# Four column orders for the moving operand of the down-projection products

## The chip, the cores and the metric

The kernel runs on one core of one Trainium2 chip. The metric is the device time of one execution in microseconds, from launch to end, median of the runs; lower is better. Beside the runs there is one profiled execution, whose span (first to last instruction) is given with its views.

## What is computed

One layer of a hybrid encoder over 256 tokens of 2048 channels, in float32. Only its last step matters for this change, the MLP with a hidden width of 8192 and a squared ReLU:

```python
x = x + merged @ w_out[i]
h2 = rms_norm(x, norm2_g[i])
x = x + jnp.square(jax.nn.relu(h2 @ w_mlp_up[i])) @ w_mlp_down[i]
```

Everything ahead of it (state-space branch, attention branch, convolution branch, gates, their merge) is the same in both kernels.

## The kernel before

All weights stream through the core once. SyncE fetches them in units of 256 rows by 512 columns (tile `raw`, 512 kB, two rows of 512 float32 on each of 128 partitions, five buffers). ScalarE copies each unit to a tile `hi` in the type fp32r (line 1208), VectorE subtracts to get the remainder `lo` (line 255); both have four buffers. Activations have been split in the same way. A product of a unit is then three passes on TensorE: activations' high part times `hi`, activations' low part times `hi`, activations' high part times `lo`.

Eight units make a block, which accumulates in one PSUM tile `main` [128, 2, 512], two banks, one per token tile of 128 tokens. There are two such tiles, so block *b* needs block *b*-2 to have been read. Blocks come in two modes. In mode "W" the weights are the stationary operand and the activations move in matmuls of 256 columns (lines 1251, 1253, 1255). In mode "X" the activations are stationary (128 by 128, a new load for each matmul) and a row of the weight tile moves, 512 contiguous float32 per partition (lines 1260, 1261, 1263): twelve matmuls per unit, two rows times two token tiles times three passes.

The MLP comes last in the stream. It is cut into four rounds of 2048 hidden channels. A round is four up-projection blocks (mode "W"; `job_up` applies the ReLU and the square and makes the tiles `ah` and `al`) and four down-projection blocks (mode "X", `down_block`, `ah` and `al` stationary). `mlp_order` puts them in the order U0 U1 D0 U2 D1 U3 D2 D3, so the groups D0 to D3 of down blocks stand apart, but for the last two. A down block ends with two additions on VectorE, one per token tile, which read the bank and add it to the residual `x` (`oacc[i]`): line 1070 for the first three rounds, line 1074 for the last, where each addition is followed by the store of 128 by 512 outputs.

The program is written out in one fixed order. A scheduler class hands out the work beside the stream by estimated engine times; its estimates, and so the order, know nothing of the order in which a matmul reads its columns. TensorE executes its matmuls in program order and takes a weight load ahead of them.

Of the kernel before, what the change touches and what calls it, by code (L numbers as in the profile page):

```python
# [21 lines left out]
T = 256  # L22
D = 2048
# [17 lines left out]

# Slabs of 4 kB per partition and PSUM banks for the work beside the weight stream.
SLOTS = 33
BANKS = 4
# Pacing of that work, in ns of engine time: the largest credit in units of the gain per weight unit, the shares
# of DVE and ACT that the weights' splitting leaves, the credit and the slabs that late work keeps free, the slack
# of the estimated clocks, and the distance between two engines.
CAP = 1.2
# [7 lines left out]
WPRIO = 1  # L56
# Weight units that are split ahead of their products.
LEAD = 3
# [20 lines left out]
class Sched:  # L79
    """Issues work beside the weight stream in portions that the engines have time for."""  # L80

# [30 lines left out]
    def _try(self, j, force):  # L112
        """Advances the job by one request; False when it has to stay."""
        if j.req is None:
# [56 lines left out]
    def require(self, cond, what):  # L171
        """Runs jobs, the most urgent first, until the condition holds."""
        level = 0
        while not cond():
            moved = False
            for j in [x for x in self.jobs if x.prio <= level]:
                while not cond() and not j.done and self._try(j, True):
                    moved = True
                if cond():
                    break  # L180
            if moved:
                level = 0
            else:
                level += 1
                if level > 9:
                    raise RuntimeError("stuck: " + what + " " + str([(j.name, j.req) for j in self.jobs])
                                       + " mem %d banks %d" % (self.mem, self.banks))
# [3 lines left out]
def kernel(ctx: ExitStack, tc: tile.TileContext, xT, xn, par, cm, cd, cq, w1, wq, ws, out):  # L191
# [27 lines left out]

    # ------------------------------------------------------------ constants  # L220
    cpar = cp.tile([P, NPAR], F32, name="cpar")
# [23 lines left out]

    # ------------------------------------------------------------ small helpers
    def natural(ap):
        """tokens in order, seen in the order of the attention: the even ones before the odd ones."""
        return ap.rearrange("p (j r) -> p r j", r=2)
# [7 lines left out]
    def add4(acc, src, first):  # L257
        """adds the four chunks of a slab to acc."""
        for k in range(4):
            if first and k == 0:  # L260
                continue
            yield "g", 700
            G.tensor_tensor(acc, src[:, 0, :] if first and k == 1 else acc, src[:, k, :], op=ALU.add)  # L263

    def rstd_steps(dst, ms, n):
        """dst = ms ** -0.5, one Newton step after the tables."""
        s = small([n], f"rs{n}", bufs=2 if n < 64 else 1)
# [17 lines left out]
    def spread(r):  # L285
        """[token, tile] to a row of all tokens on every partition, in a bank."""
        yield "m", 1
# [12 lines left out]

    # ------------------------------------------------------------ startup: x * g, rms
    def prep(kc):
        """hi and lo parts of x*g for a chunk of channels."""
        src = xt[kc // 4][:, kc % 4, :]
# [34 lines left out]
    def job_h():  # L339
        """h = x*g*rstd and its parts, for the blocks after the first."""  # L340
        yield "j", lambda: "rbc1" in st
# [21 lines left out]

    # ------------------------------------------------------------ dt
    def job_dt(main):
# [78 lines left out]

    # ------------------------------------------------------------ q, k, v of one slot (3 heads)
    qkv = {}

    def job_qk(main, off, key, gain, scaled=False):
        """three heads of q or k: per-head RMS, then transposed [e, head, token]."""
        yield "w", 1  # L450
# [67 lines left out]

    # ------------------------------------------------------------ GLU and the convolution of 31 taps
    cin, cout = [None] * 8, [None] * 4  # L520
# [17 lines left out]
    def conv_slab(i):  # L538
        """two chunks of the output of the convolution."""
        if cout[i // 2] is None:  # L540
            yield "m", 1
            cout[i // 2] = slab([4, T], name="co")
# [23 lines left out]
    def colsum(srcs, name, lhsT, ready=None):  # L566
        """sum over the channels of four [128, 4, T] slabs, on every partition, in one bank."""
        acc = small([T], "acc256", bufs=1)
# [66 lines left out]

    # ------------------------------------------------------------ xBC: convolution of 5 taps
    BT, CT, xs = [None], [None], [None] * 4

    def job_xbc(main, bi, c0):
        """bi 0: B, 1: C, 2..5: xs of group bi-2; c0: first chunk of channels in the parameters."""  # L640
        yield "m", 2
# [47 lines left out]

    # ------------------------------------------------------------ attention  # L690
    att = {}

    def job_att(j):
        """slot j: one head of each pattern, one softmax over the keys of all three. The even
        tokens stand before the odd ones, so the two dilated patterns need the keys of the queries' own tile only."""
        yield "j", lambda: all((x, j) in qkv for x in "qkv") and (j == 0 or ("done", j - 1) in att)
# [68 lines left out]

    # ------------------------------------------------------------ SSD
    y = [None] * 4
# [25 lines left out]
    def job_ssd(g, c):  # L793
        """group g, token tile c: y = D x + diagonal block of both directions + the other tile's part."""
        yield "j", lambda: cbs[g] is not None
# [79 lines left out]

    # ------------------------------------------------------------ z gate, RMS over the inner channels
    def job_z(main, g):
# [19 lines left out]
    def job_ynorm():  # L897
        """rsqrt of the mean square of y per token: the outputs of its projection are scaled by it."""
        yield "j", lambda: st["z_n"] == 4
# [19 lines left out]

    # ------------------------------------------------------------ gates, branches, merge  # L920
    sgt = {}
# [34 lines left out]
    def turn(src, h, l, gains=None):  # L956
        """hi and lo parts of a slab [token, tile, channel], with the channels on the partitions."""
        for i in range(2):
# [23 lines left out]
    def job_mhl(i):  # L982
        """parts of merged for the output projection."""
        yield "m", 2
# [8 lines left out]

    # ------------------------------------------------------------ output projection, residual, rms2
    oacc = [None] * 4
# [41 lines left out]

    # ------------------------------------------------------------ MLP
    act = {}

    def job_up(main, r, i):
# [22 lines left out]
    def job_down(main, r, i):  # L1064
        if r < 3:
            yield "j", lambda: oacc[i] is not None
            yield "w", 1
            for t in range(2):
                yield "v", 620
                V.tensor_tensor(oacc[i][:, t, :], oacc[i][:, t, :], main[:, t, :], op=ALU.add)  # L1070
            st["main_free"].add(id(main))
            return
        for t in range(2):
            V.tensor_tensor(oacc[i][:, t, :], oacc[i][:, t, :], main[:, t, :], op=ALU.add)
            nc.sync.dma_start(out[t * P:t * P + P, i * 512:i * 512 + 512], oacc[i][:, t, :])
        st["main_free"].add(id(main))
        yield "w", 0

    # ------------------------------------------------------------ the stream of weights
    st.update(h=([None] * 4, [None] * 4), ssd=([None] * 4, [None] * 4), conv=([None] * 4, [None] * 4),  # L1080
# [7 lines left out]

    def block(mode, key, post, n=512, units=8, src=None, perm=False, end=None):
        src = ws if src is None else src  # L1090
        base = used.get(id(src), 0)
        used[id(src)] = base + units
        blocks.append(dict(mode=mode, key=key, post=post, n=n, units=units, src=src, base=base, perm=perm, end=end))

# [62 lines left out]
    def down_block(r, i):  # L1157
        block("X", lambda: act[r], lambda m: [(job_down(m, r, i), 0)],
              end=(lambda: S.give(8)) if i == 3 else None)

# [10 lines left out]

    # ------------------------------------------------------------ run it
    units = [(bi, u) for bi, b in enumerate(blocks) for u in range(b["units"])]
# [41 lines left out]
    def mm(k):  # L1215
# [28 lines left out]
        for ps, e, kc, t in order:  # L1244
# [11 lines left out]
            else:  # L1256
                o = main[:, t, :n]
                xs_ = slice(t, T, 2) if b["perm"] else slice(t * P, t * P + P)
                if ps == 0:
                    PE.matmul(o, ah[:, xs_], wh[:, e, :], start=(first and e == 0), stop=False)  # L1260
                    PE.matmul(o, al[:, xs_], wh[:, e, :], start=False, stop=False)  # L1261
                else:
                    PE.matmul(o, ah[:, xs_], wl[:, e, :], start=False, stop=(last and e == 1))  # L1263
        if u == b["units"] - 1:
# [120 lines left out]
```

## Time and profile before

| | us |
|---|---|
| median of two runs | 1987.68 (1987.3 to 1988.06) |
| span of the profiled execution | 1984.9 |
| TensorE matmuls busy in it | 1969.3 |
| VectorE busy | 1315.8 |
| ScalarE busy | 1037.7 |
| GpSimd busy | 63.9 |

In the profile's rows PE is TensorE's matmuls, PEld its weight loads, DVE is VectorE, ACT ScalarE, POOL GpSimd, SP SyncE. Matmuls are pipelined: the duration of one contains the time in which its successor already runs, so what one matmul costs is the distance from its start to the next one's, not its duration. A group's row gives line, engine, operation, names and shapes of output and inputs, count, then busy time in us and mean ns of one, then the engine's idle time ahead of it. A timeline's row gives start and length in us, then the same.

### The profile page before, as it was taken

How to read it: one execution, taken by the hardware profiler on the slowest of the kernel's cores; microseconds unless marked ns; L12 is line 12 of the kernel's file. 1: busy time of each engine (PE TensorE's matmuls, PEld its weight loads, DVE VectorE, ACT ScalarE, POOL GpSimd, SP SyncE). 2: the span in 40 equal slices, each digit the busy share in tenths (PEclk: the TensorE clock that was granted, in tenths of full speed). 3: DMA queues.
4: the chain of work that ended last, by engine and by line, in shares of the span. 5: the costliest groups of instructions: out<-in, count | busy, mean ns of one | idle time of the engine just before them, and what ended most of it. 6: DMA issues, size and time to landing. Idle time of an engine off the chain costs nothing.

```text
span 1984.9 us, 29944 instructions
## 1 busy us (share of the span) xinstructions
PE 1969.3 (99%) x11788; PEld 1768.9 (89%) x11788; DVE 1315.8 (66%) x1846; ACT 1037.7 (52%) x1442; POOL 63.9 (3%) x57
## 2 busy tenths in 40 slices
PE   8999999999999999999999999999999999999998
PEld 7999999999989888888888888999988998998887
DVE  7888887877877888896655555555555554555443
ACT  6655575867666655545654444544443443344332
POOL 3000010000000000003000000000000000000000
PEclk9999999999999999999999999999999999999999
DMA  7655564555544555555555556555555555555554
GB/s 241 203 177 182 162 195 132 173 165 159 174 170 162 177 172 189 182 189 185 188 191 185 186 192 204 190 190 183 189 189 186 188 189 191 185 188 187 188 177 148
DMA packets 104766, 362.41 MB, mean 183 GB/s; under 512 B 11696, under 2 KB 12208, under 8 KB 104624
## 3 DMA queue, kind: packets, MB, share of 16 engines
q1 hardware_dynamic: 103904, 359.18, 54.4%
q8 instruction: 92, 1.51, 0.3%
q10 hardware_dynamic: 720, 1.31, 0.2%
q14 instruction: 50, 0.41, 0.1%
HBM read 358.35 MB, written 2.10 MB: 182 GB/s over the span
## 4 chain that ended last, share of the span: by engine, by line
PE 98%; POOL 1%; DMA 0%; SPq 0%; ACT 0%; issue 0%; DVE 0%; DVEq 0%; POOLq 0%
PE main L1260 20%; PE main L1261 20%; PE main L1263 20%; PE main L1253 11%; PE main L1255 11%; PE main L1251 11%; POOL acc L263 1%; PE b L839 1%; PE b L861 1%; PE b L965 1%; PE b L816 0%; DMA raw<-w_dram 0%; PE b L498 0%; PE b L754 0%; PE b L713 0%; PE b L739 0%
## 5 line engine op out<-in xcount | busy, mean ns | idle before, releaser
L255 DVE TENSOR_TENSOR lo<-raw,hi 128x1024 fp32r<-128x1024 f32 (+2 forms) x697 | 836.3, 1200 | 639.4 <-ACT hi L1208 634.1
L1208 ACT ACTIVATE hi<-raw 128x1024 fp32r<-128x1024 f32 (+2 forms) x695 | 716.7, 1033 | 872.5 <-PE main L1261 500.5
L1260 PE MATMUL main<-hi,hh 128*128 128x512 f32 (+1 forms) x800 | 304.3, 380 | 0.0
L1261 PE MATMUL main<-hi,hl 128*128 128x512 f32 (+1 forms) x800 | 298.3, 373 | 0.0
L1251 PE MATMUL main<-x2h,hi 128*128 128x256 f32 x1024 | 247.8, 281 | 0.0
L1253 PE MATMUL main<-x2l,hi 128*128 128x256 f32 x1024 | 247.3, 281 | 0.0
L1251 PE MATMUL main<-hh,hi 128*128 128x256 f32 x896 | 218.4, 283 | 0.0
L1253 PE MATMUL main<-hl,hi 128*128 128x256 f32 x896 | 216.3, 280 | 0.0
L562 DVE SCALAR_TENSOR_TENSOR co<-cin,cpar,co 128x256 f32<-128x256 f32 x480 | 208.3, 486 | 0.0
L1263 PE MATMUL main<-lo,hh 128*128 128x512 f32 (+1 forms) x800 | 201.5, 373 | 0.0
L1261 PE MATMUL main<-hi,al 128*128 128x512 f32 x512 | 201.4, 393 | 0.0
L1260 PE MATMUL main<-hi,ah 128*128 128x512 f32 x512 | 201.3, 393 | 0.0
L1251 PEld LDWEIGHTS main<-x2h,hi 128*128 128x128 f32 x1024 | 193.5, 189 | 0.2
L1253 PEld LDWEIGHTS main<-x2l,hi 128*128 128x128 f32 x1024 | 192.8, 188 | 0.2
L1261 PEld LDWEIGHTS main<-hi,hl 128*128 128x128 f32 x800 | 152.3, 190 | 22.6 <-issue 1.2
L1260 PEld LDWEIGHTS main<-hi,hh 128*128 128x128 f32 x800 | 152.1, 190 | 22.4 <-issue 0.7
L1253 PEld LDWEIGHTS main<-hl,hi 128*128 128x128 f32 x896 | 168.8, 188 | 0.7 <-issue 0.2
L1251 PEld LDWEIGHTS main<-hh,hi 128*128 128x128 f32 x896 | 168.6, 188 | 0.8 <-issue 0.2
L1263 PEld LDWEIGHTS main<-lo,hh 128*128 128x128 f32 x800 | 148.1, 191 | 22.1
L1255 PE MATMUL main<-x2h,lo 128*128 128x256 f32 x1024 | 141.8, 281 | 0.0
L1263 PE MATMUL main<-lo,ah 128*128 128x512 f32 x512 | 139.0, 393 | 0.0
L1255 PEld LDWEIGHTS main<-x2h,lo 128*128 128x128 f32 x1024 | 129.9, 189 | 0.0
(240 smaller groups left out, 2288.1 us busy)
## 6 DMA issues: line engine op xcount, KB each, us to landing
raw<-ws_dram SPq DMA_DIRECT2D x600, 512.0 KB, 3.3
raw<-wq_dram SPq DMA_DIRECT2D x88, 384.0 KB, 3.1
raw<-w_dram SPq DMA_DIRECT2D x7, 448.0 KB, 6.9
x<-xn_dram SPq DMA_DIRECT2D x4, 512.0 KB, 5.0
out_dram<-x SPq DMA_DIRECT2D x8, 256.0 KB, 3.2
xt<-xT_dram SPq DMA_DIRECT2D x7, 256.0 KB, 6.9
raw<-w_dram SPq DMA_DIRECT2D x2, 224.0 KB, 3.3
cpar<-par_dram ACTq DMA_DIRECT2D x1, 441.0 KB, 5.0
```

Of the source, the lines that this page charges most:

```text
L255: V.tensor_tensor(lo, raw, hi.bitcast(F32), op=ALU.subtract)
L263: G.tensor_tensor(acc, src[:, 0, :] if first and k == 1 else acc, src[:, k, :], op=ALU.add)
L562: V.scalar_tensor_tensor(dst[:, e, :], x[:, e, k:k + T], par_("dw", (2 * i + e) * 31 + k), dst[:, e, :], op0=ALU.mult, op1=ALU.add)
L839: PE.matmul(ba, lt, src, start=(n == 0), stop=(n == 3))
L861: PE.matmul(bd[:, i, :], em[:, 0, i, :], x[:, c, pr:pr + P], start=True, stop=True)
L1208: A.activation(h, r, AF.Copy)
L1251: PE.matmul(o, wh[:, e, cs], ah, start=(first and e == 0 and c % 2 == 0), stop=False, skip_group_check=True)
L1253: PE.matmul(o, wh[:, e, cs], al, start=False, stop=False, skip_group_check=True)
L1255: PE.matmul(o, wl[:, e, cs], ah, start=False, stop=(last and e == 1), skip_group_check=True)
L1260: PE.matmul(o, ah[:, xs_], wh[:, e, :], start=(first and e == 0), stop=False)
L1261: PE.matmul(o, al[:, xs_], wh[:, e, :], start=False, stop=False)
L1263: PE.matmul(o, ah[:, xs_], wl[:, e, :], start=False, stop=(last and e == 1))
```

## The change

The moving operand of the down-projection matmuls is read in another order than that of memory, one order for each round. Pattern 0, everywhere else, stays as it was.

| round | pattern | order in which the 512 columns of a row are streamed | step between columns |
|---|---|---|---|
| D0 | 1 | two from the first half, two from the second half, the next two from the first half, and so on | runs of 2 columns (8 bytes), then a jump between halves of about 1 kB |
| D1 | 2 | sixteen from the first half, sixteen from the second, and so on | runs of 16 columns (64 bytes), then a jump of about 1 kB |
| D2 | 3 | columns 0, 16, 32, ... 496, then 1, 17, 33, ... | every step is 16 columns, 64 bytes |
| D3 | 4 | columns 0, 2, 4, ... 510, then 1, 3, 5, ... | every step is 2 columns, 8 bytes |

The products land in the bank one after the other, so the bank holds the columns in the streamed order. The addition undoes it: it reads the bank through the inverse pattern (`walked`) and reads and writes `x` in memory order, cut into the same three or four dimensions (`like`). The same elements are added; nothing is computed more or less. The number of instructions of each engine and their order are the same in both programs; only addresses inside the 1536 down matmuls and the 32 additions differ. Comments and docstrings were also taken out, and the new helpers shift the lines behind them: 1260, 1261 and 1263 become 1295, 1296 and 1298, and 1070 and 1074 become 1102 and 1107.

```diff
+    def walk(ap, pat):
+        if pat == 1:
+            return ap.rearrange("p (h c s) -> p c h s", h=2, s=2)
+        if pat == 2:
+            return ap.rearrange("p (h c s) -> p c h s", h=2, s=16)
+        if pat == 3:
+            return ap.rearrange("p (c s) -> p s c", s=16)
+        if pat == 4:
+            return ap.rearrange("p (c s) -> p s c", s=2)
+        return ap
+
+    def walked(ap, pat):
+        if pat == 1:
+            return ap.rearrange("p (c h s) -> p h c s", h=2, s=2)
+        if pat == 2:
+            return ap.rearrange("p (c h s) -> p h c s", h=2, s=16)
+        if pat == 3:
+            return ap.rearrange("p (s c) -> p c s", s=16)
+        if pat == 4:
+            return ap.rearrange("p (s c) -> p c s", s=2)
+        return ap
+
+    def like(ap, pat):
+        if pat in (1, 2):
+            return ap.rearrange("p (h c s) -> p h c s", h=2, s=2 if pat == 1 else 16)
+        if pat in (3, 4):
+            return ap.rearrange("p (c s) -> p c s", s=16 if pat == 3 else 2)
+        return ap
...
-                V.tensor_tensor(oacc[i][:, t, :], oacc[i][:, t, :], main[:, t, :], op=ALU.add)
+                V.tensor_tensor(like(oacc[i][:, t, :], r + 1), like(oacc[i][:, t, :], r + 1),
+                                walked(main[:, t, :], r + 1), op=ALU.add)
...
-            V.tensor_tensor(oacc[i][:, t, :], oacc[i][:, t, :], main[:, t, :], op=ALU.add)
+            V.tensor_tensor(like(oacc[i][:, t, :], r + 1), like(oacc[i][:, t, :], r + 1),
+                            walked(main[:, t, :], r + 1), op=ALU.add)
             nc.sync.dma_start(out[t * P:t * P + P, i * 512:i * 512 + 512], oacc[i][:, t, :])
...
     def down_block(r, i):
         block("X", lambda: act[r], lambda m: [(job_down(m, r, i), 0)],
-              end=(lambda: S.give(8)) if i == 3 else None)
+              end=(lambda: S.give(8)) if i == 3 else None, pat=r + 1)
...
-                    PE.matmul(o, ah[:, xs_], wh[:, e, :], start=(first and e == 0), stop=False)
-                    PE.matmul(o, al[:, xs_], wh[:, e, :], start=False, stop=False)
+                    PE.matmul(o, ah[:, xs_], walk(wh[:, e, :], b["pat"]), start=(first and e == 0), stop=False)
+                    PE.matmul(o, al[:, xs_], walk(wh[:, e, :], b["pat"]), start=False, stop=False)
                 else:
-                    PE.matmul(o, ah[:, xs_], wl[:, e, :], start=False, stop=(last and e == 1))
+                    PE.matmul(o, ah[:, xs_], walk(wl[:, e, :], b["pat"]), start=False, stop=(last and e == 1))
```

More of the change, by code (lines that the diff above doesn't have):

```diff
@@ L1087, with block @@
     used = {}
-    def block(mode, key, post, n=512, units=8, src=None, perm=False, end=None):
+    def block(mode, key, post, n=512, units=8, src=None, perm=False, end=None, pat=0):
         src = ws if src is None else src
@@ L1092, in block @@
         used[id(src)] = base + units
-        blocks.append(dict(mode=mode, key=key, post=post, n=n, units=units, src=src, base=base, perm=perm, end=end))
+        blocks.append(dict(mode=mode, key=key, post=post, n=n, units=units, src=src, base=base, perm=perm, end=end,
+                           pat=pat))
     def parts(key):
```

## The prediction

> **What bounds the kernel now.** I read the page's totals first, then the chain of work that ended last, then the groups by shape for the lines that the diff touches, and last the timeline at the borders of the four rounds.
>
> ```profile
> span 1984.9 us, 29944 instructions
> PE 1969.3 (99%) x11788; PEld 1768.9 (89%) x11788; DVE 1315.8 (66%) x1846; ACT 1037.7 (52%) x1442; POOL 63.9 (3%) x57
> ...
> PE 98%; POOL 1%; DMA 0%; SPq 0%; ACT 0%; issue 0%; DVE 0%; DVEq 0%; POOLq 0%
> ```
>
> TensorE is busy 99% of the span and carries 98% of the chain. Whatever lengthens a matmul's turn lengthens the kernel by as much, and whatever slows another engine costs nothing until it becomes later than TensorE. The diff touches three groups of matmuls:
>
> ```profile
> L1261 PE MATMUL main<-hi,al 128*128 128x512 f32 x512 | 201.4, 393 | 0.0
> L1260 PE MATMUL main<-hi,ah 128*128 128x512 f32 x512 | 201.3, 393 | 0.0
> ...
> L1263 PE MATMUL main<-lo,ah 128*128 128x512 f32 x512 | 139.0, 393 | 0.0
> ```
>
> That is 3 x 512 = 1536 matmuls, 384 in each round (four blocks, eight units, twelve matmuls), with no idle time ahead of them. The 393 ns contain the overlap with the next matmul, so the price comes from the rounds' borders on the timeline (start, length):
>
> ```profile
> 1442.86 0.40 PE L1260 MATMUL main<-hi,ah 128*128 128x512 f32 x1
> ...
> 1531.89 0.28 PE L1251 MATMUL main<-x2h,hi 128*128 128x256 f32 x1
> ...
> 1622.54 0.39 PE L1260 MATMUL main<-hi,ah 128*128 128x512 f32 x1
> ...
> 1710.85 0.28 PE L1251 MATMUL main<-x2h,hi 128*128 128x256 f32 x1
> ...
> 1801.56 0.39 PE L1260 MATMUL main<-hi,ah 128*128 128x512 f32 x1
> ...
> 1890.56 0.40 PE L1260 MATMUL main<-hi,ah 128*128 128x512 f32 x1
> ...
> 1978.46 0.62 PE L1263 MATMUL main<-lo,ah 128*128 128x512 f32 x2
> ```
>
> D0 runs from 1442.86 to 1531.89 (89.03 us), D1 from 1622.54 to 1710.85 (88.31), D2 from 1801.56 to 1890.56 (89.00), D3 from there to 1978.46 + 0.62 = 1979.08 (88.52). Divided by 384, one matmul takes its turn every 0.230 to 0.232 us, and the four rounds are alike. In D2 the other engines look like this (busy us and count for PE, PEld, DVE, ACT, POOL, then granted clock, DMA share, GB/s):
>
> ```profile
> 1801.56:1890.56 89.00, 89.00 (x387) 72.23 (x386) 45.14 (x41) 35.87 (x35) 0.00 (x0) 1.00 0.56 189
> ```
>
> VectorE is half idle, ScalarE more than half, the DMA engines run at 0.56, and the clock is full. No supplier is near its limit, so a slower TensorE meets no second bound there and a TensorE at its old pace has no gap to fill.
>
> **The change, part by part.** Nothing is removed and no instruction moves. What changes is addresses, and each of the four rounds is priced by itself: its 384 matmuls times the new turn less 0.2318 us (D2's 89.00 / 384). Weight loads stay as they are, 0.19 us each, under the matmul's turn.
>
> The trace of before holds no matmul with a stepped moving operand. The nearest rows are a stepped stationary operand (tiles `xgh`, every second token, 8 bytes apart) against a contiguous one (`ah`), and a stepped VectorE instruction (line 762 reads and writes with an 8-byte step) against one with contiguous runs of 64 (line 866), both of 256 elements. Durations are ns, least, median, most:
>
> ```profile
> L1260 PEld LDWEIGHTS main<-hi,ah x512: 187/188/192, 1442.7 to 1977.8; 128*128 128x128 f32 x171
> ...
> L1260 PEld LDWEIGHTS main<-hi,xgh x96: 192/194/334, 4.4 to 69.6; 128*128 128x128 f32 x96
> ...
> L762 DVE TENSOR_TENSOR ol<-b,oh x4: 418/425/426, 117.1 to 621.2; 128x256 fp32r<-128x256 f32 x4
> ...
> L866 DVE TENSOR_TENSOR y<-y,b x16: 408/415/418, 306.8 to 733.4; 128x256 f32<-128x256 f32 x16
> ```
>
> An 8-byte step costs the weight load 194 - 188 = 6 ns over 128 columns, and VectorE 10 ns over 256 elements. That is close to free, but both are slower readers than the moving stream, which takes a column every 0.453 ns (0.2318 us / 512). How the stream behaves when it is fed more slowly is seen at two places: plain fp32 matmuls of 512 columns (line 816), and the first matmuls of the program, of 448 columns.
>
> ```profile
> 271.45 1.72 PE b L816 x4
> ```
> ```profile
> 7.36 0.58 PE L1261 MATMUL main<-hi,xgl 128*128 128x448 f32 x1
> 7.73 0.58 PE L1260 MATMUL main<-hi,xgh 128*128 128x448 f32 x1
> ```
>
> Four plain matmuls take 1.72 us on the chain, 0.43 us each; the early ones start 0.37 us apart, which for 512 columns is 0.37 x 512 / 448 = 0.423 us. Both are about half the column rate of the down rounds, for reasons of their own, and they are the slowest turns of such streams in the trace.
>
> *D1 (runs of 16, pattern 2).* 64 contiguous bytes, then a jump: 32 jumps in 512 columns. I take 0. The upper end is the weight load's 6 ns per 128 columns, 24 ns per matmul, 384 x 0.024 = 9.2 us.
>
> *D3 (8-byte step, pattern 4).* The nearest rows have this very step and cost 0.0 to 24 ns per matmul when scaled by columns; I take 0, since the weight load does not show whether its 6 ns are per column or once. The upper end is half rate, as in D2.
>
> *D0 (runs of 2, pattern 1).* Each pair stands together, as many useful bytes at one place as in D3's steps, so the same value and the same ends: 0, up to half rate.
>
> *D2 (64-byte step, pattern 3).* Here no two consecutive columns lie within 64 bytes, and no row comes near it. The lower end is 0: below nothing is excluded, because a matmul's columns cannot arrive faster than in the contiguous rows, and nothing waits less. The contiguous stream is by far the densest reader in the trace, so a fetch that brings one useful column instead of several neighbouring ones should show here if anywhere. The upper end of the forecast is half rate. The rows price it at 0.43 us (line 816), and twice the present turn is 0.464. I take the middle, 0.447: 384 x (0.447 - 0.2318) = 82.6 us, with 76 and 89 us as ends.
>
> [...]
>
> *The additions.* 32 on VectorE, which now read the bank in pieces:
>
> ```profile
> L1070 DVE TENSOR_TENSOR x<-x,main x24: 680/681/683, 1466.6 to 1892.7; 128x512 f32<-128x512 f32 x24
> ...
> L1074 DVE TENSOR_TENSOR x<-x,main x8: 680/684/689, 1912.9 to 1979.7; 128x512 f32<-128x512 f32 x8
> ```
>
> A block lasts 89.00 / 4 = 22.25 us, and its bank is needed again one block after the addition becomes possible. Two additions of 0.68 us could be ten times slower before TensorE waited, so 30 of them cost nothing. The last two stand at the very end, after the last matmul; if each doubled, the end would come 1.4 us later, and by line 762 against line 866 it is nearer 0.05 us. I take 0, ends 0 and 1.4.
>
> *What waits more.* In D2 ScalarE will wait longer for a free `hi` buffer, and VectorE and SyncE behind it. In the stretch from 1801 us to the end ScalarE already waits 88.6 us for TensorE (total us, times, longest), so this is more of the same and off the path:
>
> ```profile
> ACT hi L1208 <- PE main L1261: 88.6, 53, 1.7
> ```
>
> *Sum.* 1984.9 us of span + 0 (D0) + 0 (D1) + 82.6 (D2) + 0 (D3) + 0 (additions) = 2067.5 us of span. The median of the runs stands 1987.7 - 1984.9 = 2.8 us above the span, so the forecast is 2070.3, rounded 2070 us. With D2's two ends it is 2064 to 2077.
>
> **The rivals.**
>
> *No order costs anything.* The stream is fetched far enough ahead that steps are absorbed. For it: the 8-byte rows above cost 0 to 6 ns. Against it: those readers are slower than the stream, and 64 bytes are eight times that step. D2's turn decides: under 0.335 us the whole stays within 2% (40 us / 384 = 0.104 above 0.2318). The time would be 1984.9 + 2.8 + 0 to 1 = 1988 us. [...]
>
> *Two rounds pay.* [...] For it: the weight load's 6 ns. Against it: a loss of half the rate would be 384 x 0.215 us on top, and 6 ns is nothing like it. 1987.7 + 2 x 82.6 = 2153 us.
>
> *Everything but runs of 16 pays.* D0, D2 and D3 at half rate: 1987.7 + 3 x 82.6 = 2236 us. Same evidence, counted twice.
>
> *D2 alone, but far worse than half rate.* If one fetch must end before the next, a quarter of the rate, 0.927 us a turn: 384 x 0.695 = 267 us, 2255 us. No row of the trace is that slow.
>
> *D2 alone, a small cost.* The fetch-ahead hides a part and the turn comes to between 0.335 and 0.40 us: 40 to 65 us, 2028 to 2052 us.
>
> **How the numbers follow.** D2 alone at about half rate 0.50, nothing 0.20, two rounds 0.12, three rounds 0.07, D2 far worse 0.06, D2 a little 0.05. The forecast is the likeliest, 2070 us, with a range of its own of 2060 to 2080. The range for 8 in 10 takes in the first three and the small cost, 0.87 in all: from 1985 to 2160 us, wide because whether the step is paid at all, and by how many rounds, no row decides. Leaving out either neighbour of the forecast would leave less than 0.8 or little more. 2% of 1987.7 is 40 us, about what a measurement of this kernel can tell from no change. Slower by over 2% are all the cases but the one that costs nothing: 0.79. Within 2%: 0.20. Faster by over 2%: 0.01, since no mechanism of the change shortens a turn.
>
> **What would show it.** In the profile of the changed kernel the rounds' borders give each round's turn: I expect 0.23 us in D0, D1 and D3 and 0.43 to 0.464 us in D2, so D2 lasts 165 to 178 us. The busy time of its matmuls stays without idle time ahead; if instead TensorE shows idle time in D2, the loss is in a wait and not in the stream. The additions' median should stay near 0.68 us; over 1.4 us would be a price of its own, hidden but for the last two. In D2 VectorE's and ScalarE's busy times stay at 45 and 36 us over a longer round, and the DMA share falls to about half. The prediction is wrong if D2's turn stays under 0.335 us, if D0 or D3 leaves 0.25 us, or if the granted clock falls.

## The result and the profile after

The changed kernel took 2191.91 us (median of two, 2191.27 to 2192.55) against 1987.68 us: 1.103 times the time before, 95% interval 1.101 to 1.105. The forecast was 2070 us, with a range up to 2160. The direction was right, the size was not, and the time lies outside the range.

The page of the changed kernel, totals and chain:

```profile
span 2189.5 us, 29944 instructions
PE 2173.6 (99%) x11788; PEld 1787.6 (82%) x11788; DVE 1315.7 (60%) x1846; ACT 1036.5 (47%) x1442; POOL 63.8 (3%) x57
...
PE 98%; POOL 1%; DMA 0%; SPq 0%; ACT 0%; issue 0%; DVE 0%; DVEq 0%; POOLq 0%
```

TensorE's busy time grew by 204.3 us and the span by 204.6; VectorE (1315.7 us against 1315.8), ScalarE (1036.5 against 1037.7) and the counts stand still, and the chain is TensorE's as before (98%). Its groups of down products:

```profile
L1295 PE MATMUL main<-hi,ah 128*128 128x512 f32 x512 | 275.1, 537 | 0.0
L1296 PE MATMUL main<-hi,al 128*128 128x512 f32 x512 | 274.8, 537 | 0.0
...
L1298 PE MATMUL main<-lo,ah 128*128 128x512 f32 x512 | 208.5, 536 | 0.0
```

No idle time stands ahead of them: the matmuls themselves last longer. The mean of 537 ns is of no use, since it mixes the four rounds. The borders on the timeline part them:

```profile
1442.80 0.50 PE L1295 MATMUL main<-hi,ah 128*128 128x512 f32 x1
...
1569.82 0.29 PE L1286 MATMUL main<-x2h,hi 128*128 128x256 f32 x1
...
1660.46 0.40 PE L1295 MATMUL main<-hi,ah 128*128 128x512 f32 x1
...
2009.66 0.63 PE L1295 MATMUL main<-hi,ah 128*128 128x512 f32 x1
...
2182.83 1.08 PE L1298 MATMUL main<-lo,ah 128*128 128x512 f32 x2
```

The stretches of the four rounds, with busy us and count of PE, PEld, DVE, ACT, POOL, then clock, DMA share, GB/s:

```profile
1442.80:1569.82 127.02, 127.02 (x386) 75.04 (x385) 45.15 (x41) 36.30 (x35) 0.00 (x0) 1.00 0.41 136
1660.46:1752.62 92.16, 92.16 (x386) 73.54 (x385) 45.15 (x41) 35.80 (x35) 0.00 (x0) 1.00 0.56 183
1843.25:2009.66 166.41, 166.41 (x387) 79.19 (x385) 45.15 (x41) 36.15 (x35) 0.00 (x0) 1.00 0.31 104
2009.66:2183.91 174.25, 174.25 (x385) 79.50 (x383) 40.33 (x37) 29.60 (x28) 0.00 (x0) 1.00 0.24 82
```

| round | order | us before | us after | turn before | turn after | forecast |
|---|---|---|---|---|---|---|
| D0 | runs of 2, from the two halves | 89.03 | 127.02 | 0.232 | 0.331 | 0.232 |
| D1 | runs of 16, from the two halves | 88.31 | 92.16 | 0.230 | 0.240 | 0.230 |
| D2 | every 16th column | 89.00 | 166.41 | 0.232 | 0.433 | 0.447 |
| D3 | every 2nd column | 88.52 | 174.25 | 0.231 | 0.454 | 0.231 |

D3's stretch ends with the last matmul itself; from unit to unit its turn is 0.453 us. The four differences, 38.0 + 3.9 + 77.4 + 85.7 = 205.0 us, are the whole loss. The clock is full in all four (1.00), VectorE and ScalarE do the same work, and the additions, which now read the bank in pieces, are as fast as before: 681 and 685 ns in the median against 681 and 684 (ns, least, median, most; the second row is D3's):

```profile
L1102 DVE TENSOR_TENSOR x<-x,main x24: 678/681/684, 1476.0 to 2011.7; 128x512 f32<-128x512 f32 x24
...
L1107 DVE TENSOR_TENSOR x<-x,main x8: 679/685/689, 2053.4 to 2184.6; 128x512 f32<-128x512 f32 x8
```

### The profile page after: what moved, and what is told of

It reads as the page before. It is cut to its first block, busy times and chain, and to the rows that moved or that the text cites. A ratio compares the mean times of both kernels' runs of the same rounds, so it can differ in the third digit from the quotient of the medians.

```text
span 2189.5 us, 29944 instructions
## 1 busy us (share of the span) xinstructions
PE 2173.6 (99%) x11788; PEld 1787.6 (82%) x11788; DVE 1315.7 (60%) x1846; ACT 1036.5 (47%) x1442; POOL 63.8 (3%) x57
## 4 chain that ended last, share of the span: by engine, by line
PE 98%; POOL 1%; DMA 0%; SPq 0%; ACT 0%; issue 0%; DVE 0%; DVEq 0%; POOLq 0%
PE main L1296 21%; PE main L1295 21%; PE main L1298 21%; PE main L1288 10%; PE main L1290 10%; PE main L1286 10%; POOL acc L263 1%; PE b L839 1%; PE b L861 1%; PE b L965 0%; DMA raw<-w_dram 0%; PE b L816 0%; PE b L498 0%; PE b L754 0%; PE b L713 0%; PE b L739 0%
## 5 line engine op out<-in xcount | busy, mean ns | idle before, releaser
L1295 PE MATMUL main<-hi,ah 128*128 128x512 f32 x512 | 275.1, 537 | 0.0
L1296 PE MATMUL main<-hi,al 128*128 128x512 f32 x512 | 274.8, 537 | 0.0
L1298 PE MATMUL main<-lo,ah 128*128 128x512 f32 x512 | 208.5, 536 | 0.0
L1298 PEld LDWEIGHTS main<-lo,ah 128*128 128x128 f32 x512 | 102.5, 200 | 84.0 <-issue 60.7
L1295 PEld LDWEIGHTS main<-hi,ah 128*128 128x128 f32 x512 | 102.5, 200 | 83.9 <-issue 47.6
L1296 PEld LDWEIGHTS main<-hi,al 128*128 128x128 f32 x512 | 102.4, 200 | 83.5 <-issue 60.3
```

What stands on the lines that cost most here:

```text
L1295: PE.matmul(o, ah[:, xs_], walk(wh[:, e, :], b["pat"]), start=(first and e == 0), stop=False)
L1296: PE.matmul(o, al[:, xs_], walk(wh[:, e, :], b["pat"]), start=False, stop=False)
L1298: PE.matmul(o, ah[:, xs_], walk(wl[:, e, :], b["pat"]), start=False, stop=(last and e == 1))
```

## The experiments

All but three (`e7_split_walk`, `e10_two_halves`, `e11_both`) change only the four orders. For them the helpers took a table, one entry for each round: how the row is cut, in which order it is walked, the first column and the number of columns; the additions undo the order as before. "Turn" is the mean distance of the units' first matmuls divided by twelve. The expectations set guesses of the author's at the cause against each other, under names. The step theory is spelled out under `e3_runs`; "both theories" of the first one give D2 the turn that it had in the changed kernel. A "line" in them is four columns that begin at a multiple of four, 16 bytes, called an aligned four below. "Two-reader theory" names a guess at the cause of the 0.216 us that the first round of `e8_streams` took; no trace shows a reader, and the measured turn is what the times of `e10_two_halves` and `e11_both` are worked out from. Where no ratio stands beside a time, it is from a single execution.

```diff
-        if pat == 1:
-            return ap.rearrange("p (h c s) -> p c h s", h=2, s=2)
...
+        mem, order, sizes, o, n = SPECS[pat - 1]
+        return ap[:, o:o + n].rearrange("p (%s) -> p %s" % (mem, order), **sizes)
```

**One round alone** (`e1_d2_only`).

```diff
+    SPECS = [contiguous, contiguous, ("c s", "s c", dict(s=16), 0, 512), contiguous]
```

> Only round D2 keeps its order (64-byte step); D0, D1 and D3 stream contiguously again. Both theories: D2 0.434 us a turn as in the changed kernel, 384 x (0.434 - 0.232) = 78 us, 2065 us in all. Rival, that a stepped round disturbs what follows: D3 stays above 0.24 us a turn though its own order is contiguous.

2064.12 us, ratio 1.039 (1.036 to 1.042). D2's turn is 0.433 us, and D3's is back at 0.230. A round pays for its own order and leaves nothing behind.

**The order applied elsewhere** (`e7_split_walk`).

```diff
+                for e in range(2):
+                    es = slice(e * 512, e * 512 + 512)
+                    w = walk(r[:, es], pat)
+                    A.activation(flat(h[:, es], pat), w, AF.Copy)
+                    V.tensor_tensor(flat(l[:, es], pat), w, flat(h[:, es], pat).bitcast(F32), op=ALU.subtract)
...
-                    PE.matmul(o, ah[:, xs_], walk(wh[:, e, :], b["pat"]), start=(first and e == 0), stop=False)
+                    PE.matmul(o, ah[:, xs_], wh[:, e, :], start=(first and e == 0), stop=False)
```

> The four orders stay, but ScalarE and VectorE apply them when they split the weights (two instructions of 512 a unit instead of one of 1024 in the down rounds), and the down products stream contiguously again; bank contents and additions as in the changed kernel. If the whole loss is the order of the moving operand, the turns are 0.230 to 0.232 us in all four rounds and the time 1987 to 1990 us. Rival, that the order of the addition or the bank's contents has a part: more than 2000 us. Rival, that stepped reads on ScalarE or VectorE cost as they do on TensorE: their instructions of 512 take over 1 us, two of them come near the 2.78 us of a unit, and TensorE waits.

1986.87 us, ratio 1.000 (0.999 to 1.001). The borders of this kernel's first three down rounds (first matmul of D0, of the up round behind it, and so on to D3):

```profile
1443.16 0.40 PE L1309 MATMUL main<-hi,ah 128*128 128x512 f32 x1
...
1532.18 0.28 PE L1300 MATMUL main<-x2h,hi 128*128 128x256 f32 x1
...
1622.83 0.39 PE L1309 MATMUL main<-hi,ah 128*128 128x512 f32 x1
...
1711.14 0.28 PE L1300 MATMUL main<-x2h,hi 128*128 128x256 f32 x1
...
1801.86 0.39 PE L1309 MATMUL main<-hi,ah 128*128 128x512 f32 x1
...
1890.85 0.40 PE L1309 MATMUL main<-hi,ah 128*128 128x512 f32 x1
```

89.02, 88.31 and 88.99 us: the turns of before, with the banks and additions of the changed kernel. So the whole loss is TensorE's reading of the moving operand. ScalarE (line 1254) and VectorE (line 1255) walk the same orders in two instructions a unit. Inside the rounds D1, D2 and D3 these take (ns, least, median, most):

```profile
L1254 ACT ACTIVATE hi<-raw x46: 614/625/633, 1635.9 to 1697.1; 128x512 fp32r<-128x512 f32 x46
L1255 DVE TENSOR_TENSOR lo<-raw,hi x46: 682/689/695, 1636.8 to 1698.2; 128x512 fp32r<-128x512 f32 x46
...
L1254 ACT ACTIVATE hi<-raw x62: 1072/1108/1149, 1795.5 to 1880.0; 128x512 fp32r<-128x512 f32 x62
L1255 DVE TENSOR_TENSOR lo<-raw,hi x61: 1043/1065/1125, 1794.8 to 1878.3; 128x512 fp32r<-128x512 f32 x61
...
L1254 ACT ACTIVATE hi<-raw x60: 642/662/702, 1884.5 to 1966.9; 128x512 fp32r<-128x512 f32 x60
L1255 DVE TENSOR_TENSOR lo<-raw,hi x58: 682/686/695, 1885.5 to 1966.3; 128x512 fp32r<-128x512 f32 x58
```

Over all four rounds the means are 763 and 785 ns, which leaves about 660 and 700 for D0: an estimate from these means and the medians above. So the third rival came true by half: the step of 16 does cost these two engines, 1.108 and 1.065 us an instruction, while D3's step of 2 costs VectorE nothing (686 ns against D1's 689) and ScalarE little (662 against 625). Two instructions of D2 take 2.22 us on ScalarE and 2.13 on VectorE, which still fits under a unit's 2.78 us, and TensorE does not wait.

**The same orders in reversed rounds** (`e2_swap`).

```diff
+    SPECS = [("c s", "s c", dict(s=2), 0, 512), ("c s", "s c", dict(s=16), 0, 512),
+             ("h c s", "c h s", dict(h=2, s=16), 0, 512), ("h c s", "c h s", dict(h=2, s=2), 0, 512)]
```

> The same four orders in reversed rounds: D0 8-byte step, D1 64-byte step, D2 runs of 16, D3 runs of 2. If the price belongs to the order: 0.453, 0.433, 0.240, 0.331 us a turn and 2192 us. Rival, that it belongs to the place in the program (D3 slower than D2 in the changed kernel): D1 and D0 change by 0.02 us.

0.453, 0.433, 0.240 and 0.327 us, 2190.85 us. The price belongs to the order, not to the place. The step of 2 really is dearer than the step of 16, 0.453 us against 0.433.

**Longer runs** (`e3_runs`).

```diff
+    SPECS = [("h c s", "c h s", dict(h=2, s=s), 0, 512) for s in (4, 8, 32, 64)]
```

> Rounds D0 to D3 alternate between the two halves of a row in runs of 4, 8, 32 and 64 columns (128, 64, 16, 8 jumps in 512 columns). Step theory (each column that is not the next in memory after its predecessor costs one more column time, about 0.39 ns as in D0 with 256 jumps): turns of 0.281, 0.256, 0.238 and 0.235 us, 2020 us in all. [...]

0.252, 0.243, 0.237 and 0.230 us, 2001.3 us: not the step theory. Jumps behind runs of four columns and more cost a little: 128 of them 0.021 us above 0.231, where the 0.099 us of D0's 256 jumps would make 0.05.

**Other steps** (`e4_steps`).

```diff
+    SPECS = [("c s", "s c", dict(s=s), 0, 512) for s in (4, 8, 32, 128)]
```

> Rounds D0 to D3 stream with constant steps of 4, 8, 32 and 128 columns (16, 32, 128 and 512 bytes). Step theory: the distance does not matter, 0.43 to 0.455 us in all four, about 2305 us. Rival, that the ends of the innermost loop cost: there are 4, 8, 32 and 128 of them in 512 columns, so the last round is 0.04 to 0.05 us above the first. Rival, that distance costs: a rise from D0 to D3.

0.461, 0.431, 0.434 and 0.279 us, 2249.87 us. The longest step is by far the cheapest, so each of the three theories fell: not distance, not the loop's ends, not every step the same. With a step of 128 columns the stream runs 0, 128, 256, 384, 1, 129, ... and comes back to the same four aligned fours four times; it took 0.279 us.

**Inside an aligned four** (`e5_inline`).

```diff
+    SPECS = [("c b a", "c a b", dict(a=2, b=2), 0, 512), ("c b a", "b c a", dict(a=2, b=2), 0, 512),
+             ("c b a", "b c a", dict(a=4, b=2), 0, 512), ("", "rep", {}, 0, 512)]
```

> D0 reads each 16-byte line in the order 0, 2, 1, 3; D1 reads the first pair of every line, then the second pairs; D2 reads every second line whole, then the others; D3 reads each of 256 columns twice in a row (256 columns of each block are left out of the result there). Step theory: 384, 256, 128 jumps: 0.381, 0.331, 0.281 us; D3 0.331 if a repeat counts as a jump, 0.231 if not. [...]

0.232, 0.453, 0.232 and 0.216 us, 2068.5 us. The step theory falls with the first two rounds. Disorder inside an aligned four costs nothing beyond the contiguous stream (0.232 us), nor does every second aligned four whole (0.232), and pairs of columns, each from the next aligned four, pay the full price of D3 (0.453). Each column twice is cheaper than the contiguous stream, 0.216 us against 0.230 to 0.232.

**Offsets** (`e6_offset`).

```diff
+    SPECS = [("h c s", "c h s", dict(h=2, s=2), 1, 508), ("h c s", "c h s", dict(h=2, s=2), 0, 508),
+             ("c s", "c s", dict(c=1, s=508), 1, 508), ("h c s", "c h s", dict(h=2, s=4), 2, 504)]
```

> D0: runs of 2 from two halves of 508 columns, beginning at column 1; D1: the same beginning at column 0; D2: 508 contiguous columns from column 1; D3: runs of 4 from two halves of 504 columns beginning at column 2, so that each run lies on two 16-byte lines (4, 4, 4 and 8 columns of each block are left out of the result). [...] Step theory or a price on every visit to another line: D0 and D1 stay at 0.33 us, D3 0.28 us or more.

0.327, 0.327, 0.235 and 0.325 us for 508, 508, 508 and 504 columns, 2098.49 us. Runs of 2 from two halves of 508 columns take the same from column 1 as from column 0. Runs of 4 are cheap only if each lies on one aligned four: 0.325 us here, 0.252 in `e3_runs`.

**Columns in turn from several parts** (`e8_streams`).

```diff
+    SPECS = [("h c", "c h", dict(h=2), 0, 512), ("h c s", "c h s", dict(h=2, s=6), 0, 504),
+             ("h c", "c h", dict(h=6), 0, 504), ("h c", "c h", dict(h=8), 0, 512)]
```

> Single columns in turn from 2 (D0), 6 (D2) and 8 (D3) equal parts of the row, and runs of 6 from two halves (D1); D1 and D2 stream 504 columns and leave 8 of each block out. [...] Step theory: 0.43 us in D0, D2 and D3, 0.27 in D1.

0.216, 0.307, 0.292 and 0.487 us, 2132.67 us; the second and third are for 504 columns. The first round is the surprise: 0, 256, 1, 257, ... leaves the aligned four at every step and, at 0.216 us, is faster than the contiguous stream. At every second place of this stream stand 0, 1, 2, 3, ...; with the changed kernel's step of 2 (D3) there stand 0, 4, 8, ..., and with its runs of 2 (D0) 0, 256, 2, 258. The next kernel takes new orders by what stands at every second place.

**New orders, chosen by every second place** (`e9_groups`).

```diff
+    SPECS = [("c a b", "c b a", dict(a=2, b=4), 0, 512), ("h c s", "c h s", dict(h=4, s=2), 0, 512),
+             ("h c s", "s c h", dict(h=2, s=2), 0, 512), ("c b a", "b c a", dict(b=8, a=4), 0, 512)]
```

> [...] D0: 0, 4, 1, 5, 2, 6, 3, 7 in every eight columns (each step changes the line): 0.216 us, below the contiguous 0.232. [...] D2: 0, 256, 2, 258, 4, 260 and so on, then the odd columns: 0.23 us, though the step of 2 alone took 0.453. D3: every eighth line whole, then the next: 0.23 us. About 2070 us. Step theory: 0.43 us or more in D0 and D2. [...]

0.216, 0.445, 0.232 and 0.242 us, 2067.58 us: D0 and D2 as expected, D3 0.01 us above. D1 streams pairs in turn from the four quarters of the row (0, 1, 128, 129, 256, ...). At every second place stand 0, 1, 2, 3 in D0, 0, 128, 256, 384 in D1, 0, 2, 4, 6 in D2 and 0, 2, 32, 34 in D3. The sharpest pair stands in two earlier kernels. D0 of the changed kernel streams 0, 1, 256, 257, 2, 3, 258, 259, ...; D0 of `e8_streams` streams 0, 256, 1, 257, 2, 258, 3, 259, .... Every four columns are the same, only the two in the middle are swapped. From one unit's first matmul to the next unit's, first the changed kernel, then `e8_streams`:

```profile
1502.36 0.51 PE L1295 MATMUL main<-hi,ah 128*128 128x512 f32 x1
...
1506.37 0.50 PE L1295 MATMUL main<-hi,ah 128*128 128x512 f32 x1
```
```profile
1500.99 0.38 PE L1288 MATMUL main<-hi,ah 128*128 128x512 f32 x1
...
1503.58 0.38 PE L1288 MATMUL main<-hi,ah 128*128 128x512 f32 x1
```

4.01 us a unit against 2.59: the swap takes a third off the time. At every second place it turns 0, 256, 2, 258 into 0, 1, 2, 3.

**The order that is faster than contiguous, in use** (`e10_two_halves`, `e11_both`). Both start from the kernel before. The weights lie in memory with each row's even columns first, so the bank comes out in natural order.

```diff
+    def inturn(ap):
+        return ap.rearrange("p (r j) -> p j r", r=2)
...
-                    PE.matmul(o, ah[:, xs_], wh[:, e, :], start=(first and e == 0), stop=False)
+                    PE.matmul(o, ah[:, xs_], inturn(wh[:, e, :]), start=(first and e == 0), stop=False)
...
+def _halves(p):
+    k, _, n = p.shape
+    order = np.concatenate([np.arange(0, n // 2, 2), np.arange(1, n // 2, 2)])
+    return p.reshape(k, P, 2, n // 2)[..., order].reshape(k, P, n)
```

> The kernel before, with every product whose moving operand is a weight row (q, k, v, z, gates, branches, output and down projections) streamed from the two halves of the row in turn (0, 256, 1, 257, ...); the weights lie in memory with the even columns first, so the bank is in natural order and nothing else changes. Two-reader theory: 0.216 us instead of 0.231 for 512 columns, 4320 x 0.015 = 65 us, and 0.0125 us less for each of 1056 matmuls of 384, 13 us: 1909 us. Rival, that other engines set the pace once TensorE is faster, in the first half above all: 1930 to 1980 us. Step theory: far slower than before.

> As e10_two_halves, and the activations of the second norm are stored with the even tokens first and streamed from their two halves in turn in the up projections (256 columns). Two-reader theory: 0.109 us instead of 0.118 for 256 columns, 3072 x 0.009 = 27 us less than e10_two_halves, 1882 us. Rival, that the fixed part of a matmul of 256 columns sets 0.118: the same time as e10_two_halves.

1907.83 us, ratio 0.960 (0.9585 to 0.9614), and 1888.33 us, ratio 0.950 (0.9485 to 0.9517). In `e11_both` the additional edit stores the activations of the second norm with even tokens first:

```diff
-                    A.activation(h[:, 2 * i + e, :], b[:, e, :], AF.Copy, scale=gains(2 * i + e))
+                    A.activation(o_(h[:, 2 * i + e, :]), i_(b[:, e, :]), AF.Copy, scale=gains(2 * i + e))
...
-                        PE.matmul(o, wh[:, e, cs], ah, start=(first and e == 0 and c % 2 == 0), stop=False,
+                        PE.matmul(o, wh[:, e, cs], mv(ah), start=(first and e == 0 and c % 2 == 0), stop=False,
```

Sixteen matmuls of 256 columns take there

```profile
1350.37 0.28 PE L1259 MATMUL main<-x2h,hi 128*128 128x256 f32 x1
...
1352.15 1.06 PE L1263 MATMUL main<-x2h,lo 128*128 128x256 f32 x8
```

1.78 us, 0.111 us each against 0.118 before (an up round of before: 90.65 us / 768); 0.109 was expected, hence 19.5 us instead of 27. TensorE is still the bound at 99% of the span (`e11_both`):

```profile
PE 1869.8 (99%) x11788; PEld 1741.3 (92%) x11788; DVE 1314.4 (70%) x1846; ACT 1034.9 (55%) x1442; POOL 64.9 (3%) x57
```

## Why the prediction was wrong

The forecast's sum for the rounds was 82.6 us against 205.0: short by 38.0 in D0, 3.9 in D1 and 85.7 in D3, too long by 5.2 in D2.

**D2's size was right, its reason only in part.** Half rate was forecast at 0.447 us a turn and 82.6 us; measured 0.433 and 77.4. The row of plain fp32 matmuls, 0.43 us, was the better of the two ends, but no run shows that the two have a common cause. "One useful column instead of several neighbouring ones" does not set D2 apart: D3 streams two columns of an aligned four one after the other and pays as much, 0.453 us. That a fetch brings several columns and runs ahead was the author's guess, there and in the rivals; no run shows a fetch.

**D3 is the step that failed most.** "I take 0, since the weight load does not show whether its 6 ns are per column or once" left out 85.7 us. The weight load reads 128 columns in 0.19 us, the moving stream 512 in 0.23; that a reader of a third of the pace passes 8-byte steps says nothing about the faster one. VectorE's row has the same limit. It was right about VectorE, which in `e7_split_walk` paid for D2's step and not for D3's (1065 and 686 ns), just the forecast's split; for TensorE the two turns are 0.433 and 0.453 us.

**D0 failed with it.** It was set to D3's value. "As many useful bytes at one place as in D3's steps, so the same value" counted bytes in a place. D0 cost 38.0 us, between nothing and half rate, and by the measured prices it and D3 are different cases.

**Faster than contiguous.** "A matmul's columns cannot arrive faster than in the contiguous rows" is wrong as well: two halves in turn took 0.216 us (`e8_streams`). This did not hurt the forecast, since none of the four orders is of that kind.

**D1** was taken at 0 with 9.2 us as its end and cost 3.9. **The additions** were taken at 0 and cost nothing (681 and 685 ns in the median). **The cover** held: nothing but TensorE moved, in either direction.

**The rivals.** "Two rounds pay" stood at 2153 us with a chance of 0.12, "everything but runs of 16" at 2236 us. The truth is between, because D0 pays half, a size that no rival had. The range ended below it, since three paying rounds were given 0.07 on evidence that spoke of slower readers only.

**What the runs put in its place.** The price is a property of the moving read alone (`e7_split_walk`: 1986.87 us with the orders in the splitting), paid by each round for itself (`e1_d2_only`: D2 0.433 us, D3 0.230) and independent of place (`e2_swap`: 0.453, 0.433, 0.240 and 0.327 us in reversed rounds). No trace shows how a row is read, so no cause stands here. One property of the order itself sorts the runs: whether each column shares its aligned four with the column two places before or behind it in the stream.

| order | shares | measured turn, us | run |
|---|---|---|---|
| two halves in turn | all | 0.216 | `e8_streams` |
| 0 4 1 5 2 6 3 7 | all | 0.216 | `e9_groups` |
| each column twice | all | 0.216 | `e5_inline` |
| contiguous | all | 0.230 to 0.232 | `before` |
| runs of 64, 32, 8, 4 from two halves | all | 0.230, 0.237, 0.243, 0.252 | `e3_runs` |
| 0 2 1 3 in each aligned four | all | 0.232 | `e5_inline` |
| every 2nd aligned four whole | all | 0.232 | `e5_inline` |
| 0 256 2 258 ..., then the odd columns | all | 0.232 | `e9_groups` |
| contiguous from column 1 (508 columns) | all but two | 0.235 | `e6_offset` |
| D1, runs of 16 | all | 0.240 | `after` |
| every 8th aligned four whole | all | 0.242 | `e9_groups` |
| runs of 6 (504 columns) | two thirds | 0.307 | `e8_streams` |
| step of 128 | none | 0.279 | `e4_steps` |
| six parts in turn (504 columns) | none | 0.292 | `e8_streams` |
| runs of 4 from column 2 (504 columns) | none | 0.325 | `e6_offset` |
| D0, runs of 2 | none | 0.327 to 0.331 | `e2_swap`, `e6_offset`, `after` |
| steps of 8, 16, 32 | none | 0.431, 0.433, 0.434 | `e4_steps`, `after` |
| pairs from four quarters | none | 0.445 | `e9_groups` |
| D3, step of 2, and pairs one aligned four apart | none | 0.453 | `after`, `e5_inline` |
| step of 4 | none | 0.461 | `e4_steps` |
| eight parts in turn | none | 0.487 | `e8_streams` |

Where all columns share, a turn took 0.216 to 0.252 us; where none does, 0.279 to 0.487; runs of 6 lie between. The sorting was made from these runs, those of `e9_groups` being the only ones whose orders were chosen by it, and it gives no size within a group: why four parts in turn (the step of 128) cost 0.279 us and eight 0.487, or why the contiguous stream takes 0.015 us more than two halves in turn, no run shows.

## What to carry to other kernels

Price a moving operand's order by its own measured turn, not by stepped reads of slower engines: here one and the same step of 8 bytes was free for VectorE (686 ns in `e7_split_walk`, 689 for runs of 16), cost a weight load 6 ns and nearly doubled the matmul's turn, 0.453 us against 0.231. Where a permutation is needed, apply it where there is slack (here the splitting on ScalarE and VectorE, at no cost to the kernel, though in D2 their instructions took over 1 us instead of 0.6 to 0.7) and let TensorE stream whole aligned fours (every second one 0.232 us, runs of 4 0.252; runs of 4 that straddle two 0.325). Where TensorE is the bound and data can be laid out freely, try streaming the two halves of a row in turn: it took 4% off a kernel that read contiguously, and 5% with the up projections included. All of this is measured on fp32r rows; other types were not tried.

## What the hardware showed unexpectedly

The contiguous float32 stream is not the fastest one: 0.230 to 0.232 us for 512 columns, against 0.2158 us when two contiguous halves alternate or each column is read twice, at the same granted clock (0.998 in `before`, `e5_inline` and `e8_streams`). A step of 512 bytes that returns to the same four aligned fours took 0.279 us, a step of 8 bytes 0.453.
